# A recurrence's key norms once per 512 tokens, its triangular inverse by 16x16 blocks, and new waits in the plan of TensorE's order

## The chip, the cores and the metric

The kernel runs on one core of a Trainium2 chip. The metric is the device time of one execution in microseconds. A core has TensorE (PE; its weight loads are shown as PEld), VectorE (DVE), ScalarE (ACT), GpSimd (POOL) and SyncE (SP, which issues all DMAs of this kernel). Each engine works through its own instructions in one fixed order. A difference of about 0.2% is what a measurement of this kernel can tell from none.

## The reference

One decoder layer on 2048 tokens of width 1024, in fp32. `h` is the normed input and `z = h @ W_in`. Branch A is RWKV-7 with 8 heads of 64 channels: for each head and token a state `S` is decayed, corrected and read. Branch B is a causal pooling mixer. Both are gated, merged and projected; then come a squared-ReLU MLP, an embedding gate and a norm. The part that the change touches:

```python
kk = heads(k * f32(k_k))
kk = kk / jnp.maximum(jnp.linalg.norm(kk, axis=-1, keepdims=True), L2_EPS)

def rwkv7_step(S, inp):
    r, w, k, v, kk, a = inp
    sa = jnp.einsum('bhvk,bhk->bhv', S, -kk)
    S = (S * w[:, :, None, :]
         + sa[..., None] * (kk * a)[:, :, None, :]
         + v[..., None] * k[:, :, None, :])
    y = jnp.einsum('bhvk,bhk->bhv', S, r)
    return S, y
```

## The kernel before

**Stages.** The tokens are four blocks of 512. Stage A of a block (`stage_A`) makes `z` from the normed input in 128-column pieces; each dense product is three fp32r matmuls (high by high, low by high, high by low parts), and 24 of them fill one PSUM tile `d`. It writes `r|k|v` and the low-rank parts to DRAM as `zD`, and the pooling branch and gates to `thD` and `mbD`. Stage B (`stage_B`) merges the branches and projects them. Then come the MLP and the embedding in two halves of 1024 tokens, which hold no recurrence.

**The recurrence.** It runs in 32 units of 64 tokens, all heads at once: 4 pairs of heads, a pair filling the 128 partitions. Within a unit the steps of 64 tokens are one triangular system, solved by matrices:

- `prep0` loads `zs` from `zD` and makes `kx = k * k_k` and its square `sq`. `prep_a` sums the squares per head (four matmuls with `hsel`), takes `rsqrt` on 8 partitions, and splits the result into `rd`. `prep` spreads it by a matmul with `hbr` and scales `kx`.
- `prep` then makes the products `bdb·AR` (masked by DVE into `Ast`, line 783) and `bdk·AR`, and transposes `bdv` and `BK`. The unit's diagonal blocks of 32x32 go from `Ast` to DRAM (`aD`).
- `invert` loads them as `At`, each 32x32 block on several partitions, and inverts them on DVE: one elimination of pairs of rows (`Apr`), then 16 pairs of a product `Xtmp` (line 869) and a reduction into `Xt` (line 872), over 2, 4, ... 32 columns. `Xt` goes to DRAM (`xD`) and from there in six DMAs into the block-diagonal tile `xd`.
- `chain` is the serial part: `TL·SV` gives `Tn`; `xd·Tn` (even halves) gives `U`; `aof·U` is subtracted from `Tn` by DVE (line 911); `xd·Tn` (odd halves) gives `VU`; `NB·VU` gives the next state `SV`; `RD·SV + Ct·VU` gives the output `Y`. `gnorm` norms `Y` and transposes it (`ybd`).

**What sets the order.** TensorE's order is written out in advance by `drive`: generators for dense work and for the units' parts yield, and a clock in Python (`clock`, advanced by every `mm`) decides which goes on. Behind each step a part yields the time, from the table `LAT`, that must pass on this clock before its next step; dense products fill it. `pace` is the least distance of units. The other engines' orders are set by the framework's scheduler, with the units' instructions at high priority. The recurrence's PSUM tiles come from two rings of two buffers: `rps` (tiles `rp`: all of `prep`) and `cps` (tiles `rc`: `chain`).

Of the kernel before, what the change touches and what calls it, by code (L numbers as in the profile page):

```python
# [10 lines left out]
F32 = mybir.dt.float32  # L11
# [20 lines left out]
NSPLIT = P // (2 * 2 * PC)  # L32
MCOL = SUB // NSPLIT
# [10 lines left out]
           hop=3.1, hu=2.8, hv=5.3, hs=3.0, inv=47.1, gn=17.8, pace=34.4, pace2=31.5)  # L44
# [3 lines left out]
RDK = SUB + 2 * NP  # L48
# [50 lines left out]
def hybrid_kernel(ctx, tc, consts, x, p, g_mix, w_in, mu_shift, w0, w_decay_up, a0, w_aaa_up,  # L99
# [13 lines left out]
    mbD = dram.tile([P, 8, T], F32, name="mbD")  # L113
    yaD = dram.tile([P, NPAIR, T], F32, name="yaD")
# [13 lines left out]
    def mm(out_, lhsT, rhs, start, stop, **kw):  # L128
        n = 1
        for d in rhs.shape[1:]:  # L130
            n *= d
        clock[0] += max(0.107, n * (4 if rhs.dtype == F32 else 1) / 2370.0)
        PE.matmul(out_, lhsT, rhs, start=start, stop=stop, **kw)  # L133
# [62 lines left out]
    with ExitStack() as c1:  # L196
# [136 lines left out]
        ACT.copy(out=bor, in_=raw[:, 0:P])
        hbr = rw.tile([RDK, P], FR, name="hbr")
        POOL.memset(hbr.bitcast(F32), 0.0)
        for o in (0, SUB):
            ACT.copy(out=hbr[o:o + 2 * NP, :], in_=raw[0:2 * NP, P:])
        rd = rw.tile([RDK, W1], FR, name="rd")
        POOL.memset(rd.bitcast(F32), 0.0)
# [5 lines left out]
        bd["aof"] = static([P, PC // 2, P], "aof", 2)  # L345

# [57 lines left out]
        def stage_A(b, nxt):  # L404
# [238 lines left out]
        aD = [dram.tile([4 * PC, SUB, SUB], F32, name=f"aD{i}") for i in range(2)]  # L643
        xD = [dram.tile([4 * PC, SUB, SUB], F32, name=f"xD{i}") for i in range(2)]
# [20 lines left out]
        carried = {}  # L665

        def prep0(i):
# [8 lines left out]
            sq = wt("sq")  # L676
            ACT.activation(out=sq, in_=kx, func=AF.Square)
            return zs, kx, sq

        def prep_a(i):  # L680

            u, g = divmod(i, NG)
            zs, kx, sq = p0.pop(i)
# [7 lines left out]
            ps = rps()  # L691
# [3 lines left out]
            ss = rw.tile([2 * NP, UT], F32, name="kss", bufs=1)  # L695
            DVE.tensor_scalar(ss, ps[0:2 * NP, 0:UT], 1e-24, None, op0=ALU.max)
# [26 lines left out]
            rk2 = rw.tile([P, W1], F32, name="rk2", tag="sq", bufs=1)  # L723
# [6 lines left out]
            return zs, kx, Ei, E, k2, rkr  # L730
# [7 lines left out]
        def prep(i):  # L738
            u, g = divmod(i, NG)
            par = i % 2  # L740
            zs, kx, Ei, E, k2, rkr = pa.pop(i)
# [9 lines left out]
            mm(ps[:, W1:2 * W1], hbr, rd, True, True)  # L751
# [6 lines left out]
            DVE.tensor_tensor(kk, kx, ps[:, W1:2 * W1], ALU.mult)  # L758
# [19 lines left out]

            ps = rps()
# [5 lines left out]
            for h in range(2):  # L785
                for d in range(2):
                    hd = h * 2 + d
                    rows = slice(h * L + d * SUB, h * L + (d + 1) * SUB)
                    SP.dma_start(out=ad[hd * PC:(hd + 1) * PC].rearrange("q s t -> s q t"),  # L789
                                 in_=Ast[rows, :, d * SUB:(d + 1) * SUB])  # L790
            chain_ready[i] = clock[0] + LAT["inv"]
# [38 lines left out]
            xdr = xD[par]  # L830
            for h in range(2):
                for d in range(2):
                    hd = h * 2 + d
                    lo = h * L + d * SUB
                    xv3 = xdr[hd * PC:(hd + 1) * PC].rearrange("q j i -> j q i")
                    for to, fr in ((ALLQ, ALLQ),) if d == 0 else ((EVEN, ODD), (ODD, EVEN)):
                        SP.dma_start(out=xd[lo:lo + SUB, to, lo:lo + SUB], in_=xv3[:, fr, :])
            carried[i] = dict(dl=dl, TL=TL, RD=RD, SV=SV, VU=VU, Ct=Ct, aof=aof, xd=xd, NB=NB, gg=gg, bon=bon)

        def invert(i):  # L840
            par = i % 2
            ad, xdr = aD[par], xD[par]


            Atp = rw.tile([P, SUB * (SUB + 1)], F32, name="At", bufs=1)
            Atf = Atp[:, 0:SUB * SUB]
            At = Atf.rearrange("p (s t) -> p s t", t=SUB)
            SP.dma_start(out=Atf, in_=ad.rearrange("q s t -> q (s t)").unsqueeze(1).broadcast_to(
                [4 * PC, NSPLIT, SUB * SUB]))

            lvl = 1
            while lvl < FS:
                nb = SUB // (2 * lvl)
                Ab = At.rearrange("p s (b r) -> p s b r", r=2 * lvl)
                dgv = Atp.rearrange("p (c w) -> p c w", w=2 * lvl * (SUB + 1))
                for e in range(lvl):
# [150 lines left out]
        def drive(dg):  # L1007
            gate, at, dense_on = None, 0.0, True
            while dense_on or active or counts["gn_done"] < NU:
                admit()  # L1010
                ready = [a for a in active if a[3] <= clock[0] and (a[4] is None or a[4]())]
                if ready:
                    a = min(ready, key=lambda a: (a[0] != "chain", a[3]))
                    a[4] = None
                    try:
                        with tc.high_priority():
                            lat = next(a[2])
                        if lat is None:
# [340 lines left out]
```

## Time and profile before

| | |
|---|---|
| median of 3 runs | 3357.87 us (3354.74 to 3360.87) |
| the profiled execution | 3362.13 us, its span 3360.3 us |
| TensorE's mean granted clock | 0.98 |
| DMA traffic | 485.60 MB, mean 145 GB/s |
| costliest waits on DMA issue | SP for `Xt` before `xD`: 112.6 us in 19 waits |

The profile's page gives busy time by engine; a matmul's end is modelled, so a busy PE is not PE at its peak. In its views a row is: line, engine, operation, output tile <- input tiles, shape, count, then busy us and mean ns of one, then the idle time of the engine just before and what ended it. A wait called "issue" is one for which the profile shows no releaser. A timeline row begins with its start and its length in us, and ends with the idle time ahead of it in brackets.

### The profile page before, as it was taken

How to read it: one execution, taken by the hardware profiler on the slowest of the kernel's cores; microseconds unless marked ns; L12 is line 12 of the kernel's file. 1: busy time of each engine (PE TensorE's matmuls, PEld its weight loads, DVE VectorE, ACT ScalarE, POOL GpSimd, SP SyncE). 2: the span in 40 equal slices, each digit the busy share in tenths (PEclk: the TensorE clock that was granted, in tenths of full speed). 3: DMA queues.
4: the chain of work that ended last, by engine and by line, in shares of the span. 5: the costliest groups of instructions: out<-in, count | busy, mean ns of one | idle time of the engine just before them, and what ended most of it. 6: DMA issues, size and time to landing. Idle time of an engine off the chain costs nothing.

```text
span 3360.3 us, 43232 instructions
## 1 busy us (share of the span) xinstructions
PE 3196.8 (95%) x15177; PEld 2620.5 (78%) x15177; DVE 2021.1 (60%) x5020; ACT 1182.4 (35%) x2406; POOL 950.1 (28%) x1162
## 2 busy tenths in 40 slices
PE   7989999999999997889899999999999999999998
PEld 6777777777878786668688888888788888888887
DVE  4489888788887879873643333333775333333375
ACT  4445544554455444431322222211332222221132
POOL 4655444344434435421111111111102111111110
PEclk9999999999999998999999999999999999999999
DMA  8866767666766567778741111110233111111021
GB/s 249 243 216 205 245 205 236 222 212 186 227 218 219 175 209 235 234 242 290 275 140 51 51 51 51 44 51 26 83 131 113 51 51 51 51 47 47 26 65 60
DMA packets 391030, 485.60 MB, mean 145 GB/s; under 512 B 168158, under 2 KB 298268, under 8 KB 367644
## 3 DMA queue, kind: packets, MB, share of 16 engines
q1 hardware_dynamic: 390812, 482.83, 45.1%
q8 instruction: 120, 1.97, 0.2%
q14 instruction: 98, 0.80, 0.1%
HBM read 363.21 MB, written 119.54 MB: 144 GB/s over the span
## 4 chain that ended last, share of the span: by engine, by line
PE 70%; DVE 14%; DMA 7%; ACT 3%; issue 3%; POOL 2%; SPq 1%; DVEq 0%; POOLq 0%; ACTq 0%
PE d L133 63%; DVE Xtmp L869 3%; PE rc L133 3%; PE rp L133 3%; DMA At<-aD 2%; DVE Xt L872 1%; ACT sq L961 1%; DMA aD<-Ast 1%; DMA wf<-wc 1%; DMA t2k<-yaD 1%; PE rp L137 1%; DVE wf L238 1%; DVE Apr L859 1%; PE rc L137 1%; SPq L789 0%
## 5 line engine op out<-in xcount | busy, mean ns | idle before, releaser
L133 PE MATMUL d<-big,wf 128*128 128x512 f32 (+1 forms) x3288 | 840.6, 403 | 17.6 <-DVE wf L238 9.2
L133 PEld LDWEIGHTS d<-big,wf 128*128 128x128 f32 x3288 | 608.9, 192 | 150.2 <-DVE wf L238 11.7
L133 PE MATMUL d<-wf,rt 128*128 128x512 f32 x3072 | 722.4, 395 | 0.0
L133 PE MATMUL d<-hT,wf 128*128 128x512 f32 x3072 | 700.1, 389 | 0.6 <-DVE hT L185 0.4
L133 PEld LDWEIGHTS d<-wf,rt 128*128 128x128 f32 x3072 | 574.9, 187 | 139.7
L133 PEld LDWEIGHTS d<-hT,wf 128*128 128x128 f32 x3072 | 576.5, 188 | 121.6 <-DVE hT L185 0.7
L1099 POOL TENSOR_TENSOR wf<-wr,wf 128x512 fp32r<-128x512 f32 x146 | 256.8, 1764 | 1396.1 <-ACT wf L1095 1394.5
L1215 DVE TENSOR_TENSOR xa<-xa,d 128x512 f32<-128x512 f32 x256 | 175.7, 686 | 410.0 <-PE d L133 409.6
L1095 ACT CAST wf<-wr 128x1024 fp32r<-128x1024 f32 x148 | 153.4, 1045 | 688.7 <-PE d L133 570.0
L1159 DVE TENSOR_TENSOR t<-t,d 128x512 f32<-128x512 f32 x128 | 87.9, 687 | 274.9 <-ACT t L1158 274.9
L869 DVE TENSOR_TENSOR Xtmp<-Xt,At 128x16 f32<-128x16 f32 (+15 forms) x512 | 238.3, 465 | 9.3
L133 PE MATMUL d<-yx,wf 128*128 128x512 f32 x768 | 210.0, 420 | 25.7 <-ACT yx L387 15.8
L133 PE MATMUL d<-wf,big 128*128 128x512 f32 x768 | 190.5, 401 | 11.0 <-DVE t2k L608 9.2
L1158 ACT ACTIVATE t<-d 128x512 f32<-128x512 f32 x128 | 76.6, 599 | 347.3 <-PE d L133 347.3
L133 PEld LDWEIGHTS d<-yx,wf 128*128 128x128 f32 x768 | 150.1, 202 | 62.1 <-ACT yx L387 17.5
L1099 DVE TENSOR_TENSOR wf<-wr,wf 128x512 fp32r<-128x512 f32 (+1 forms) x148 | 115.8, 783 | 131.3 <-ACT wf L1095 130.9
L133 PE MATMUL d<-wf,hT 128*128 128x512 f32 x768 | 183.6, 394 | 0.0
L1161 DVE TENSOR_TENSOR rt<-t,rt 128x512 fp32r<-128x512 f32 x128 | 154.0, 1203 | 45.3 <-ACT rt L1160 45.3
L133 PEld LDWEIGHTS d<-wf,big 128*128 128x128 f32 x768 | 143.0, 191 | 43.7 <-DVE t2k L608 11.1
L133 PEld LDWEIGHTS d<-wf,hT 128*128 128x128 f32 x768 | 143.9, 188 | 33.6
L872 DVE TENSOR_REDUCE Xt<-Xtmp 128x8 f32<-128x16 f32 (+15 forms) x512 | 147.5, 288 | 9.4
L238 POOL TENSOR_TENSOR wf<-wr,wf 128x640 fp32r<-128x640 f32 (+2 forms) x69 | 121.1, 1756 | 76.4 <-ACT wf L235 71.8
(225 smaller groups left out, 3921.3 us busy)
## 6 DMA issues: line engine op xcount, KB each, us to landing
wf<-wc SPq DMA_DIRECT2D x131, 1024.0 KB, 5.7
wr<-in_w_ff_dram SPq DMA_DIRECT2D x128, 512.0 KB, 4.0
wc<-wf SPq DMA_DIRECT2D x50, 1024.0 KB, 6.3
wr<-in_w_in_dram SPq DMA_DIRECT2D x51, 512.0 KB, 4.4
zD<-t2k SPq DMA_DIRECT2D x96, 256.0 KB, 4.7
zs<-zD SPq DMA_DIRECT2D x32, 640.0 KB, 6.4
At<-aD SPq DMA_DIRECT2D x32, 512.0 KB, 4.8
xt<-in_x_dram SPq DMA_DIRECT2D x28, 512.0 KB, 6.9
```

Source lines behind the costliest of these rows:

```text
L133: PE.matmul(out_, lhsT, rhs, start=start, stop=stop, **kw)
L137: PE.transpose(out_, in_, idn)
L238: eng.tensor_tensor(wf[:, 1, c], raw[:, c], hi.bitcast(F32)[:, c], ALU.subtract)
L859: DVE.tensor_tensor(pr, Ab[:, :, :, e:e + 1].broadcast_to([P, SUB, nb, lvl]), dgv[:, :, o:o + lvl].unsqueeze(1).broadcast_to([P, SUB, nb, ...
L869: DVE.tensor_tensor(tmp[:, :, :, 0:n], Xt[:, :, 0:n].unsqueeze(2).broadcast_to([P, MCOL, FS, n]), At[:, 0:n, r:n].rearrange("p s r -> p r ...
L872: DVE.tensor_reduce(Xt[:, :, r:n].unsqueeze(3), tmp[:, :, :, 0:n], AX.X, ALU.add)
L1095: ACT.copy(out=hi, in_=raw[:, 0:k * n])
L1099: eng.tensor_tensor(wf[:, 1, c], raw[:, c], hi.bitcast(F32)[:, c], ALU.subtract)
L1158: ACT.activation(out=t, in_=ps, func=AF.Relu)
L1159: DVE.tensor_tensor(t, t, ps, ALU.mult)
L1161: DVE.tensor_tensor(rt[:, 1, cs], t, rt[:, 0, cs].bitcast(F32), ALU.subtract)
L1215: DVE.tensor_tensor(xa[j][:, ns], xa[j][:, ns], ps, ALU.add)
```

## The change

Three things change, and with them the plan.

1. **Key norms.** The squares of the keys are taken in stage A, for 512 tokens at once: `key_squares` has the squares as the weight and two columns (`hsel`, now the heads' masks) as the moving operand, `key_norms` takes `rsqrt` of 128x32 values, transposes them and writes 8 rows to DRAM (`kD`). `prep0` reads them back, each row to 64 partitions (`kb`). The per-unit `sq`, `rsqrt` and `rd` go.
2. **The inverse.** Only the 16x16 diagonal blocks are inverted on DVE (8 pairs in place of 16), after 8 small DMAs to `aD` in place of 4. The off-diagonal 16x16 squares (`Of`, masked by POOL from `Ast`) are filled in on TensorE: `Of·Xr` (`Xr` is `Xc` transposed by DVE) is copied into `xd` by ACT with a minus sign, then `ident·Xc + xd·Xc` is copied into `xd` by ACT, in six pieces. `xD` and its DMAs go. `invert` becomes a generator with two steps on TensorE, and both take their PSUM tile from `rps`.
3. **The plan.** `mm` costs an fp32 product max(0.22, n/595) and an fp32r product max(0.11, n/2260); the wait behind `aof·U` is now `ht = 6.5` (it was `hu = 2.8`); `hv` goes from 5.3 to 5.8 and `hs` from 3.0 to 3.5; `inv` is 28.0 up to `Of·Xr`, then `z = 2.8` and `X = 3.5`. A unit's `bdb·AR` may not go ahead of the `Of·Xr` of the unit before.

The diff, cut to its core:

```diff
-LAT = dict(..., hop=3.1, hu=2.8, hv=5.3, hs=3.0, inv=47.1, gn=17.8, pace=34.4, pace2=31.5)
+LAT = dict(..., hop=3.1, hu=2.8, ht=6.5, hv=5.8, hs=3.5, inv=28.0, z=2.8, X=3.5, gn=17.8, pace=34.4, pace2=31.5)
...
-        clock[0] += max(0.107, n * (4 if rhs.dtype == F32 else 1) / 2370.0)
+        clock[0] += max(0.22, n / 595.0) if rhs.dtype == F32 else max(0.11, n / 2260.0)
...
+            def key_squares(j, sq):
+                ps = dps()
+                for c in range(TB // P):
+                    mm(ps[:, 2 * c:2 * c + 2], sq[:, c * P:(c + 1) * P], hsel, True, True)
+                DVE.tensor_scalar(kss[:, :, 2 * j:2 * j + 2], ps[:, 0:n].rearrange("p (c h) -> p c h", h=2), 1e-24, None,
+                                  op0=ALU.max)
+                if j == NPAIR - 1:
+                    late.append(lambda ri=rsqrt(fg, kss.rearrange("p c h -> p (c h)"), TB // P * n, "k", bufs=1): key_norms(ri))
+            def key_norms(ri):
+                ps = dps()
+                for c in range(TB // P):
+                    tr(ps[0:n, c * P:(c + 1) * P], ri[:, c * n:(c + 1) * n], ident)
+                rt = t2k()
+                ACT.copy(out=rt[0:n, :], in_=ps[0:n, :])
+                SP.dma_start(out=kD[:, t0:t0 + TB], in_=rt[0:n, :])
...
+            kb = wt("kb", 2)
+            for h, hp in enumerate(hps):
+                SP.dma_start(out=v3(kb)[hp], in_=kD.rearrange("(j h) t -> h j t", h=2)[h, :, t0:t0 + UT].unsqueeze(
+                    0).broadcast_to([L, NP, UT]))
...
-            for j in range(NP):
-                mm(ps[0:2 * NP, 0:UT], hsel[:, 2 * (NP - 1 - j):2 * (2 * NP - 1 - j)], sq[:, j * UT:(j + 1) * UT],
-                   j == 0, j == NP - 1)
...
-            ri = rsqrt(rw, ss, UT, "k", rows=2 * NP, bufs=1)
...
-            mm(ps[:, W1:2 * W1], hbr, rd, True, True)
...
-            DVE.tensor_tensor(kk, kx, ps[:, W1:2 * W1], ALU.mult)
+            DVE.tensor_tensor(kk, kx, kb, ALU.mult)
...
+            yield lambda: of_read[0] >= i - 1
...
-                    SP.dma_start(out=ad[hd * PC:(hd + 1) * PC].rearrange("q s t -> s q t"),
-                                 in_=Ast[rows, :, d * SUB:(d + 1) * SUB])
+            for b in range(P // SB):
+                SP.dma_start(out=ad[b].rearrange("q s t -> s q t"),
+                             in_=Ast[b * SB:(b + 1) * SB, :, b * SB % L:b * SB % L + SB])
+            Of = bd["Of"][0]
+            for lo in range(0, P, SUB):
+                rows = slice(lo, lo + SUB)
+                POOL.tensor_tensor(Of[rows, :, rows], Ast[rows, :, lo % L:lo % L + SUB],
+                                   omask[rows].unsqueeze(1).broadcast_to([SUB, PC, SUB]), ALU.mult)
...
-            for r in range(0, SUB, FS):
+            for r in range(0, SB, FS):
...
-            SP.dma_start(out=xdr.rearrange("q (k m) i -> (q k) (m i)", m=MCOL), in_=Xt.rearrange("p m i -> p (m i)"))
+            Xc = rw.tile([P, PC, SUB], F32, name="Xc", bufs=1)
+            DVE.tensor_tensor(Xc.rearrange("p q (c t) -> p q c t", t=SB), Xt.unsqueeze(2).broadcast_to([P, PC, 2, SB]),
+                              cmask.unsqueeze(1).unsqueeze(3).broadcast_to([P, PC, 2, SB]), ALU.mult)
+            Xr = rw.tile([P, PC, SUB], F32, name="Xr", tag="Xtmp", bufs=1)
+            DVE.transpose(Xr.rearrange("p q t -> p (q t)"), Xc.rearrange("p q t -> p (q t)"))
+            yield LAT["inv"]
+            Of, xd = bd["Of"][0], bd["xd"][par]
+            yield lambda: counts["chain_done"] >= i - 1
+            ps = rps()
+            for q in range(PC):
+                mm(ps[:, q * SUB:(q + 1) * SUB], Of[:, q, :], Xr[:, q, :], True, True)
+            for lo in range(0, P, SUB):
+                ACT.activation(out=xd[lo:lo + SUB, :, lo:lo + SUB], in_=v3(ps[:, 0:PC * SUB], SUB)[lo:lo + SUB],
+                               func=AF.Copy, scale=-1.0)
+            of_read[0] = i
+            yield LAT["z"]
+            ps = rps()
+            mm(ps[:, 0:PC * SUB], ident, Xc.rearrange("p q t -> p (q t)"), True, False)
+            for q in range(PC):
+                mm(ps[:, q * SUB:(q + 1) * SUB], xd[:, q, :], Xc[:, q, :], False, q == PC - 1)
+            pv = v3(ps[:, 0:PC * SUB], SUB)
+            for lo in range(0, P, SUB):
+                for to, fr in ((ALLQ, ALLQ),) if lo % L == 0 else ((EVEN, ODD), (ODD, EVEN)):
+                    ACT.copy(out=xd[lo:lo + SUB, to, lo:lo + SUB], in_=pv[lo:lo + SUB, fr, :])
+            chain_ready[i] = clock[0] + LAT["X"]
...
             DVE.tensor_tensor(Tn, Tn, ps[:, 0:W1], ALU.subtract)
-            yield LAT["hu"]
+            yield LAT["ht"]
```

The order of instructions moves in three places. In these rows a tile's name carries its number, a matmul's inputs are the moving and then the stationary operand, and x is how many of a kind follow each other.

TensorE, from `aof·U` to the second `xd·Tn` of a unit in the midst of stage A, first as it was:

```order
L133 MATMUL rc<-U,aof_242 128x128 x2
L133 MATMUL d<-big,wf 128x512 x12
L133 MATMUL d<-yx,wf 128x512 x3
L133 MATMUL rc<-Tn,xd_236 128x128 x2
L133 MATMUL d<-yx,wf 128x512 x9
```

The same place of another unit in stage A now:

```order
L130 MATMUL rc<-U,aof_239 128x128 x2
L130 MATMUL d<-yx,lrw 128x512 x3
L130 MATMUL d<-big,wf 128x512 x6
L134 MATMUL rp<-ident,ybd_235 128x128 x4
L130 MATMUL d<-big,wf 128x512 x18
L130 MATMUL rc<-Tn,xd_233 128x128 x2
```

Fifteen dense products stood between the two; now 27 do, and the transposes of `ybd`.

TensorE around `bdb` and `bdk`, which take the two buffers `rp` in turn, before:

```order
L133 MATMUL d<-big,wf 128x512 x9
L133 MATMUL rp<-AR,bdb_226 128x128 x4
L133 MATMUL d<-big,wf 128x512 x3
L133 MATMUL rp<-AR,bdk_228 128x128 x4
L133 MATMUL d<-big,wf 128x512 x12
L137 MATMUL rp<-ident,bdv_230 128x128 x4
```

And now, with the two new steps of `invert` ahead of them:

```order
L130 MATMUL rp<-Xr,Of_241 128x32 x4
L130 MATMUL d<-yx,lrw 128x512 x3
L130 MATMUL d<-big,wf 128x512 x12
L130 MATMUL rp<-Xc,ident 128x128
L130 MATMUL rp<-Xc,xd_231 128x32 x4
L130 MATMUL rp<-AR,bdb_221 128x128 x4
L130 MATMUL rp<-AR,bdk_223 128x128 x4
L130 MATMUL d<-big,wf 128x512 x9
```

`bdk` took the buffer that `bor` had filled some way ahead; now it takes the one that `xd·Xc` has filled just ahead of `bdb`. In 20 of the 32 units the three stand in this order in the ring.

DVE around the subtraction that makes the second `Tn` of a unit (line 911), before:

```order
L872 TENSOR_REDUCE Xt<-Xtmp 128x4x2
L869 TENSOR_TENSOR Xtmp<-Xt,At 128x8x30
L872 TENSOR_REDUCE Xt<-Xtmp 128x4x2
L869 TENSOR_TENSOR Xtmp<-Xt,At 128x256
L911 TENSOR_TENSOR Tn<-Tn,rc 128x256
L872 TENSOR_REDUCE Xt<-Xtmp 128x4x2
```

And now (the subtraction is line 936):

```order
L859 TENSOR_TENSOR Apr<-At 128x392
L861 TENSOR_TENSOR At<-At,Apr 128x4x14x7
L450 SCALAR_TENSOR_TENSOR t2k<-ze,vec,t2k 128x512
L936 TENSOR_TENSOR Tn<-Tn,rc 128x256
L862 MEMSET At 128x4x16
L868 TENSOR_TENSOR Xtmp<-Xt,At 128x8x2
```

It stood behind ten or more of the 16 products of the next unit's inverse in 24 of 32 units; now it stands ahead of that inverse or near its head, in 18 units behind `Apr`, which is the first to wait for the DMA of `At`.

More of the change, by code (lines that the diff above doesn't have):

```diff
@@ L31 @@
 SUB = 32
-NSPLIT = P // (2 * 2 * PC)
-MCOL = SUB // NSPLIT
+SB = SUB // 2
 TB = 512
@@ L327, in static @@
             return r
-        raw = fg.tile([P, 2 * P], F32, name="craw", tag="t2k", bufs=5)
+        raw = fg.tile([P, P], F32, name="craw", tag="t2k", bufs=5)
         SP.dma_start(out=raw, in_=consts[:, C_BO:])
         bor = rw.tile([P, P], FR, name="bor")
[L333 to L339, printed above, removed]
+        ACT.copy(out=bor, in_=raw)
         bd = {}
@@ L480, in stage_A @@
                 which, j = divmod(zi, NPAIR)
+                if late:
+                    late.pop(0)()
+                    yield
+                if which == 1:
+                    sq = t2k()
+                    ACT.activation(out=sq, in_=zs, func=AF.Square, scale=col("kk", j))
+                    late.append(lambda j=j, sq=sq: key_squares(j, sq))
                 ps = dps()
@@ L740, in prep @@
             par = i % 2
-            zs, kx, Ei, E, k2, rkr = pa.pop(i)
+            zs, kx, kb, Ei, E, k2, rkr = pa.pop(i)
             r_ = zs[:, 0:NP, :]
@@ L841, in invert @@
             par = i % 2
[L842 to L856, printed above, removed]
-                    pr = rw.tile([P, SUB, nb, lvl], F32, name="Apr", tag="Xtmp", bufs=1)
-                    o = e * SUB + lvl
-                    DVE.tensor_tensor(pr, Ab[:, :, :, e:e + 1].broadcast_to([P, SUB, nb, lvl]),
-                                      dgv[:, :, o:o + lvl].unsqueeze(1).broadcast_to([P, SUB, nb, lvl]), ALU.mult)
-                    DVE.tensor_tensor(Ab[:, :, :, lvl:2 * lvl], Ab[:, :, :, lvl:2 * lvl], pr, ALU.add)
-                lvl *= 2
@@ L863, in invert @@
-            DVE.memset(Atf[:, 0:SUB * SUB:SUB + 1], 1.0)
-            Xt = rw.tile([P, MCOL, SUB], F32, name="Xt", bufs=1)
-            POOL.tensor_copy(Xt.rearrange("p m i -> p (m i)"), x0t)
-            tmp = rw.tile([P, MCOL, FS, SUB], F32, name="Xtmp", tag="Xtmp", bufs=1)
-            for r in range(0, SUB, FS):
+            Atf = rw.tile([P, PC * SB * SB], F32, name="At", bufs=1)
+            SP.dma_start(out=Atf, in_=aD[par].rearrange("b q s t -> b (q s t)").unsqueeze(1).broadcast_to(
+                [P // SB, SB, PC * SB * SB]))
@@ new lines, in invert @@
+            At = Atf.rearrange("p (q s t) -> p q s t", q=PC, t=SB)
+            Ad = Atf.rearrange("p (q w) -> p q w", q=PC)
+            nb = SB // FS
+            Ab = Atf.rearrange("p (q s b r) -> p q s b r", q=PC, s=SB, r=FS)
+            ns = SB - FS
+            pr = rw.tile([P, PC, ns, nb - 1], F32, name="Apr", tag="Xtmp", bufs=1)
+            step = FS * (SB + 1)
+            DVE.tensor_tensor(pr, Ab[:, :, 0:ns, 1:, 0], Ad[:, :, step + 1:SB * SB - SB:step].unsqueeze(2).broadcast_to(
+                [P, PC, ns, nb - 1]), ALU.mult)
```

106 lines of the change are left out of this document (45 added, 61 removed).

## The prediction

> **What bounds the kernel now.** I read the head of the page first, then busy time by stretch. The columns of the second view are the stretch and its length in us, then busy time and instructions of PE, PEld, DVE, ACT, POOL, and last the granted clock of PE, the DMA share and GB/s.
>
> ```profile
> span 3360.3 us, 43232 instructions
> PE 3196.8 (95%) x15177; PEld 2620.5 (78%) x15177; DVE 2021.1 (60%) x5020; ACT 1182.4 (35%) x2406; POOL 950.1 (28%) x1162
> ```
>
> ```profile
> 160.00:1290.00 1130.00, 1055.58 (x5577) 873.28 (x5575) 949.43 (x2771) 584.81 (x1362) 495.22 (x779) 0.97 0.68 213
> 1290.00:1600.00 310.00, 263.60 (x1294) 216.66 (x1294) 221.46 (x555) 107.54 (x253) 102.25 (x117) 0.93 0.76 254
> 1764.00:3361.00 1597.00, 1584.47 (x6985) 1290.05 (x6983) 689.67 (x1343) 370.46 (x599) 241.16 (x137) 1.00 0.19 58
> ```
>
> TensorE is the bound, and its instructions run in one fixed order. Behind 1764 us it idles 13 of 1597 us at full clock; the change does not touch that part. Between 160 and 1600 us, where the 32 units of the recurrence run between the dense products of stages A and B, PE idles 74 + 46 = 120 us, its clock is below 1, and DVE is 84% busy in the first stretch. So time can come only from PE's idle gaps there and the slow clock behind them; whatever TensorE is given to do in addition is paid in full. Next, who ended the gaps: the waits of PE (us in total, times, longest), and the grouped row of the chain's products with `xd` (busy, mean ns, then idle before).
>
> ```profile
> PE d L133 <- DVE t2k L608: 16.1, 6, 6.9
> PE d L133 <- DVE wf L238: 9.2, 4, 4.6
> PE rc L133 <- DVE VU L918: 9.0, 3, 5.8
> ```
>
> ```profile
> L133 PE MATMUL rc<-Tn,xd 128*128 128x128 f32 x256 | 44.5, 300 | 55.0 <-issue 34.4 <-DMA xd<-xD 10.2 <-ACT zp L509 4.9
> ```
>
> The largest wait, 55 us, stands before `xd·Tn`, and its releaser is mostly unnamed ("issue"). The timeline of one unit names it:
>
> ```profile
> 940.30 0.61 PE L133 MATMUL rc<-U,aof 128*128 128x128 f32 x4
> 945.56 0.68 PE L133 MATMUL rc<-Tn,xd 128*128 128x128 f32 x4 [1.21 <-issue]
> 944.10 1.03 DVE L869 TENSOR_TENSOR Xtmp<-Xt,At 128x256 f32<-128x256 f32 x1
> 945.05 0.41 DVE L911 TENSOR_TENSOR Tn<-Tn,rc 128x256 f32<-128x256 f32 x1
> ```
>
> `aof·U` is over at about 940.7, but the subtraction that makes the new `Tn` starts at 945.05: it stands in DVE's queue behind the inverse of the next unit (16 pairs of L869 and L872). The plan gives this hop 2.8 us of other matmuls. So PE waits for DVE's order, not for arithmetic.
>
> **The change, part by part.** Sums are against the profiled execution: 3362.1 us, of which the span is 3360.3; the median shown, 3357.9, is 4.3 lower.
>
> *1. TensorE's own work.* In the timeline the next start gives a group's cost; an fp32 product leaves two records, so x8 is four products.
>
> ```profile
> 600.92 0.61 PE L133 MATMUL rp<-sq,cst 128*8 128x64 f32 x8
> 601.46 0.66 PE L137 MATMUL rp<-ident,BK 128*128 128x128 f32 x4
> ...
> 626.36 4.38 PE L133 MATMUL d<-big,wf 128*128 128x512 f32 x18
> 630.58 0.40 PE L133 MATMUL rp<-rkr,bor 128*128 128x256 f32 x2
> 630.91 0.38 PE L133 MATMUL rp<-rd,hbr 40*128 40x256 f32 x1
> 631.22 1.97 PE L137 MATMUL d<-ident,xt 128*128 128x128 f32 x16
> ...
> 637.28 1.06 PE L133 MATMUL rp<-AR,bdb 128*128 128x128 f32 x8
> 638.09 0.94 PE L133 MATMUL d<-yx,wf 128*128 128x512 f32 x3
> ```
>
> ```profile
> L133 PEld LDWEIGHTS rp<-sq,cst 128*8 128x8 f32 x256 | 13.8, 89 | 10.4 <-issue 9.9 <-DVE gss L949 0.4
> L133 PEld LDWEIGHTS rc<-SV,RD 128*128 128x128 f32 x256 | 39.5, 195 | 0.0
> ```
>
> Removed per unit: `sq` 0.54 and `rd` 0.31 us. Added per unit: four `Of·Xr`, one with `ident`, four `xd·Xc`: 9 products, 18 records. No row has a 128-column weight with only 32 moving columns. From below it is half of a `sq` record (0.54/8/2 = 0.034 us: half the columns), from above a `bor` record (0.33/2 = 0.165). I take the `bdb` record, 0.81/8 = 0.101, because the weight is as wide, and the load of 128 columns takes 195 - 89 = 106 ns more than that of 8: narrow moving data does not make the load cheaper. That is 18 x 0.101 - 0.85 = +0.97 us, +31 in 32 units. Key norms per block: 16 products with 2 columns and four transposes (0.49, a quarter of the 1.97 us row), 32 x 0.101 + 0.49 = 3.7, four blocks +15. **+46** (ends -2 and +91).
>
> [...]
>
> *2. The hop before the second `xd`.* `ht` is 6.5 where `hu` gave 2.8: mostly 27 dense products stand there in place of 15, work that is due anyway, so the wait costs nothing as long as dense work is left. And in the new DVE order `Tn` stands at the head of the next inverse or before it, where it stood behind ten or more pairs in most units. I leave 6 of the 55 us; the 10.2 for the `xd` DMA goes with `xD`: **-49** (-55 to -35).
>
> *3. The clock behind the gaps.*
>
> ```profile
> 705.25 0.68 PE L133 MATMUL rc<-Tn,xd 128*128 128x128 f32 x4 [3.51 <-issue]
> 705.69 5.97 PE L133 MATMUL d<-big,wf 128*128 128x512 f32 x18
> 711.50 0.40 PE L133 MATMUL rp<-rkr,bor 128*128 128x256 f32 x2
> ```
>
> 18 dense products take 630.58 - 626.36 = 4.22 us undisturbed (part 1) and 711.50 - 705.69 = 5.81 behind a gap of 3.5 us: 1.6 more. Thirteen gaps of 2 us or more go by parts 2 and 5 (nine at the second `xd`, the DMA's, three of the waits for DVE): **-21** (-30 to -8).
>
> [...]
>
> *4. A new wait: the PSUM ring `rp`, two buffers.* In 20 of 32 units the order is: `xd·Xc` into one buffer, the four `bdb` into the other, then `bdk`, which needs the first again. Six ACT copies must have read it; before, `bdk` followed `rkr·bor`, long drained. ACT's rows:
>
> ```profile
> 892.33 3.70 PE L133 MATMUL d<-big,wf 128*128 128x512 f32 x15
> 892.61 0.75 ACT L887 COPY Tn<-rc 64x256 f32<-64x256 f32 x2 [0.46 <-PE rc L133]
> 897.90 1.06 ACT L906 COPY VU<-rc 32x128 f32<-32x128 f32 x4
> ```
>
> ACT starts 0.28 us after PE moves on; a copy of 32x128 takes 0.265; two such and four of half the columns, at 0.2 (an estimate between half and whole), make 0.28 + 1.33 = 1.6, with the semaphore back some 1.8. PE has 0.81 (`bdb`) to hide it. Behind `bdk` wait `bdv`, the next chain step and all dense work. **+20** (20 x 1.0; 0 to 42, the upper end with one 0.5-us and longer instruction ahead on ACT).
>
> *5. DVE's load.* Busy us and mean ns of one:
>
> ```profile
> L869 DVE TENSOR_TENSOR Xtmp<-Xt,At 128x16 f32<-128x16 f32 (+15 forms) x512 | 238.3, 465 | 9.3
> L872 DVE TENSOR_REDUCE Xt<-Xtmp 128x8 f32<-128x16 f32 (+15 forms) x512 | 147.5, 288 | 9.4
> L155 DVE SCALAR_TENSOR_TENSOR rs_yk<-rs_qk,rs_yk 8x64 f32<-8x64 f32 x96 | 27.3, 284 | 0.2
> ```
>
> The sixteen pairs of a unit take (238.3 + 147.5)/32 = 12.1 us. The eight of 144 to 256 elements go, those of 16 to 128 stay; they are more than half of it, and I take 7.5 us. So go the nine steps of the key rsqrt, 9 x 0.28 = 2.5; the product for `Xc` and the transpose come, some 0.5 each (128 elements, near the mean of the first row). About -9 a unit, some 290 us of the 1171 in the two stretches. It shortens no path of its own; it shows in the waits for DVE. Of 16.1 + 9.0 = 25.1 us of PE's waits I let two thirds go, since most of that queue was the inverse: **-17** (-25 to 0). SP no longer stands waiting for `Xt` with weight loads behind it, so of the 9.2 us for `wf` half goes: **-5** (-9 to 0). POOL (four small products for `Of`, the `rd` product gone) and ACT (ten copies, some 2.4 us a unit, one square gone) stay near half busy; what they delay is in part 4.
>
> *6. The new inverse's path.* First SP, then DVE, then PE:
>
> ```profile
> 879.37 2.27 SPq L789 DMA_DIRECT2D aD<-Ast  x4
> 892.72 1.13 DVE L859 TENSOR_TENSOR Apr<-At 128x512 f32<-128x512 f32 x1
> 910.43 0.42 DVE L872 TENSOR_REDUCE Xt<-Xtmp 128x8 f32<-128x256 f32 x1
> 877.18 1.05 PE L133 MATMUL rp<-AR,bdb 128*128 128x128 f32 x8
> 1271.47 1.05 PE L133 MATMUL rp<-AR,bdb 128*128 128x128 f32 x8
> 1296.29 1.13 DVE L859 TENSOR_TENSOR Apr<-At 128x512 f32<-128x512 f32 x1
> ```
>
> Here `Apr` starts 15.5 us after `bdb`, and the block ends 18.1 later with other work between. Eight pieces to `aD` in place of four delay it by 2.3; the block loses 7.5 and the key steps between: about 9 remain. So `Xr` is ready some 27 us behind `bdb`; in the new order some 93 dense products at 0.234 (4.22/18), 22 us, and 8 us of the recurrence's own groups stand between `bdb` and `Of·Xr`. In stage B it is not enough: at 1271 `Apr` came 24.8 behind. Four units there could wait 7 us each; DVE's shorter queue, in which that `Apr` stood, takes part of it: **+8** (0 to 40).
>
> Sum: 46 - 49 - 21 + 20 - 17 - 5 + 8 = **-18**: 3344 for the profiled execution, **3340** on the scale of the median.
>
> **The rivals.** *The DMA at DVE's head (slower).* In 18 units `Tn` now stands behind `Apr`, which waits for `At`. `aof·U` comes 33 dense products and some 5 us of small groups behind the next `bdb`, 13 us, and the second `xd` 7 later; so an `At` beyond some 20 us stalls PE there, and `Of·Xr` behind it. Against it: 15.5 above, plus 2.3. For it: 24.8 in stage B. At 22.5 everywhere 18 units pay 2.5 us: that is 45 us more, 3385. *The loads cost more (slower).* At the `bor` record, 0.165, term 1 is +91 in place of +46: 3385; it decides from 0.127 a record on, where 704 added records have eaten the 18 us. *Nothing is won.* The ring's `bdk` waits 2 us in place of 1, behind an ACT cast or activation: +20, 3360, no change. *More is won.* Term 1 near 20 since the moving columns are few, and no late `Xr`: some -52 in all, 3306. That the shorter inverse does nothing and only `ht` works is possible: then the -17 falls away and the time is 3357.
>
> **How the numbers follow.** Forecast 0.45; more won 0.15; no change, by either way, 0.15; the DMA at DVE's head 0.13; dear loads 0.12. A measurement tells about 0.2% (7 us) from no change. Faster 0.60, same 0.15, slower 0.25. The range leaves out a tail on each side: 3292 to 3384; the likeliest case alone is 3318 to 3351.
>
> **What would show it.** Right: PE's idle before `Tn,xd` falls from 55 to under 10; `rp` products with `Of`, `ident` and `xd` add some 58 us of PE work, near 0.1 a record; DVE falls by some 300 us; PE waits before `bdk` for ACT's `xd` copies, about 1 us, 20 times. Wrong: `Apr <- DMA At` grows far beyond its present share and `Tn` starts behind it; `Of·Xr` waits for `Xr` outside stage B; records of 0.16; or `bdk` waits of 2 us and more.

## The result and the profile after

The changed kernel takes 3496.18 us (median of 4 runs, 3492.57 to 3499.65) against 3357.70 of the kernel before: ratio **1.041** (95% interval 1.039 to 1.043). It is 4.1% slower, 156 us above the forecast of 3340 and above the range (3292 to 3384).

The head of its page, and busy time by stretch (the columns are those of the prediction):

```profile
span 3490.8 us, 43424 instructions
...
PE 3263.9 (94%) x15609; PEld 2694.0 (77%) x15609; DVE 1759.6 (50%) x4124; ACT 1256.5 (36%) x2712; POOL 941.2 (27%) x1257
```

```profile
160.00:1290.00 1130.00, 996.12 (x5331) 839.28 (x5330) 675.80 (x1841) 597.47 (x1493) 451.75 (x792) 0.94 0.63 190
...
1895.00:3491.00 1596.00, 1583.84 (x6980) 1289.17 (x6978) 686.30 (x1343) 370.67 (x599) 241.12 (x137) 1.00 0.18 58
```

The last stretch is as it was (13 us idle of some 1597), so the 130 us that the span grew stand ahead of it, where the recurrence runs. There TensorE did less in the same 1130 us (996 us busy, 1056 before) at a clock of 0.94 (0.97), although DVE was busy for 676 us in place of 949. By the head, the span grew by 130.5 us: 67.1 us of TensorE's busy time and 63.4 of its idle time (226.9 against 163.5 us).

The groups of TensorE and then of DVE that answer to the prediction (busy us, mean ns | idle ahead of them and what ended it):

```profile
L130 PE MATMUL rc<-Tn,xd 128*128 128x128 f32 x256 | 42.5, 291 | 32.1 <-ACT Tn L912 21.1 <-DVE At L862 6.2 <-DVE Tn L936 2.9
L130 PE MATMUL rp<-AR,bdk 128*128 128x128 f32 x256 | 37.3, 291 | 13.2 <-ACT xd L897 9.8 <-ACT sq L986 3.0 <-POOL rk L734 0.4
...
L130 PE MATMUL rp<-Xc,xd 128*128 128x32 f32 x256 | 32.2, 270 | 5.1 <-ACT xd L886 5.1
L130 PE MATMUL rp<-Xr,Of 128*128 128x32 f32 x256 | 31.3, 266 | 0.0
...
L130 PE MATMUL rp<-Xc,ident 128*128 128x128 f32 x64 | 12.4, 276 | 3.1 <-DVE Ast L793 3.1
...
L859 DVE TENSOR_TENSOR Apr<-At 128x392 f32<-128x392 f32 x32 | 29.1, 909 | 220.5 <-DMA At<-aD 220.5
```

The releaser "issue" ahead of `rc<-Tn,xd` is gone, but 32.1 of the 55.0 us are still there: 21.1 ahead of the first `xd·Tn` of two units, for ACT's copy `Tn`, and 11.0 in all ahead of the second (44.9 before). What stands out is the last row: DVE stood **220.5 us** at `Apr`, 6.9 per unit on average, for the load of `At`. Before, the same row said:

```profile
L859 DVE TENSOR_TENSOR Apr<-At 128x512 f32<-128x512 f32 x32 | 40.6, 1268 | 51.6 <-DMA At<-aD 51.4
```

One unit of the changed kernel, with a wait longer than the average, shows the path, SP first, then DVE (start, length):

```profile
589.21 7.15 SPq L796 DMA_DIRECT2D aD<-Ast  x8
596.46 0.38 SPq L840 DMA_DIRECT2D gg<-zD  x1
596.94 0.58 SPq L990 DMA_DIRECT2D yaD<-sq  x1
597.61 1.28 SPq L698 DMA_DIRECT2D kb<-kD  x2
599.06 0.60 SPq L849 DMA_DIRECT2D At<-aD  x1
...
588.49 0.69 DVE L793 TENSOR_TENSOR Ast<-rp,mk 128x512 f32<-128x512 f32 x1
...
611.31 0.91 DVE L859 TENSOR_TENSOR Apr<-At 128x392 f32<-128x392 f32 x1 [8.86 <-DMA At<-aD]
```

`Ast` is done at 589.2, the eight pieces are issued by 596.4, `At` goes out at 599.1, and `Apr` starts 12.2 us later (median of the 32 units 8.2). DVE has nothing it may do for 8.9 us of that, since its order is fixed; dense evictions stand behind `Apr`. In the page's chain of the work that ended last, the load of `At` has 5% of the span; before it had 2%. Finally some of TensorE's longest waits:

```profile
PE d L130 <- DMA wf<-wc: 31.0, 11, 7.8
PE rc L130 <- ACT Tn L912: 21.1, 2, 11.2
...
PE d L130 <- DVE t2k L629: 19.2, 6, 5.7
```

The first was 2.5 us before, the last 16.1. Summed over all rows of TensorE, the idle time ahead of the chain's products (tiles `rc`) fell from 74.8 to 53.1 us; ahead of the units' other products (`rp`) it rose from 4.3 to 28.8, and ahead of dense work (`d`) from 75.1 to 135.9.

### The profile page after: what moved, and what is told of

Its sections match the earlier page's. It is cut to its first block, busy times and chain, and to the rows that moved or that the text cites. A ratio compares the mean times of both kernels' runs of the same rounds, so it can differ in the third digit from the quotient of the medians.

```text
span 3490.8 us, 43424 instructions
## 1 busy us (share of the span) xinstructions
PE 3263.9 (94%) x15609; PEld 2694.0 (77%) x15609; DVE 1759.6 (50%) x4124; ACT 1256.5 (36%) x2712; POOL 941.2 (27%) x1257
## 4 chain that ended last, share of the span: by engine, by line
PE 66%; DMA 15%; DVE 8%; ACT 3%; issue 3%; POOL 3%; SPq 1%; DVEq 0%; POOLq 0%; ACTq 0%
PE d L130 60%; DMA At<-aD 5%; PE rp L130 3%; PE rc L130 2%; DMA wf<-wc 2%; DMA zs<-zD 1%; DMA aD<-Ast 1%; ACT sq L986 1%; DVE bdb L772 1%; DMA t2k<-thD 1%; DMA zD<-t2k 1%; DMA wc<-wf 1%; SPq L796 1%; DVE Xtmp L868 1%; PE rc L134 1%
## 5 line engine op out<-in xcount | busy, mean ns | idle before, releaser
L130 PE MATMUL d<-big,wf 128*128 128x512 f32 (+1 forms) x3288 | 854.5, 409 | 50.8 <-DMA wf<-wc 30.4
L130 PEld LDWEIGHTS d<-big,wf 128*128 128x128 f32 x3288 | 620.5, 196 | 186.5 <-DMA wf<-wc 35.3
L130 PE MATMUL d<-yx,wf 128*128 128x512 f32 x768 | 205.1, 414 | 32.8 <-ACT yx L379 12.9
L130 PE MATMUL d<-wf,big 128*128 128x512 f32 x768 | 193.1, 406 | 22.7 <-DVE t2k L629 19.2
L859 DVE TENSOR_TENSOR Apr<-At 128x392 f32<-128x392 f32 x32 | 29.1, 909 | 220.5 <-DMA At<-aD 220.5
L986 ACT ACTIVATE sq<-rp,vec 64x64 f32<-64x64 f32 x256 | 102.5, 401 | 60.1 <-PE rp L134 56.9
```

The lines of the kernel that those rows point to most:

```text
L986: ACT.activation(out=yo[hp, q * UT:(q + 1) * UT], in_=ps[hp, q * P:(q + 1) * P][:, hp], func=AF.Identity, scale=col("lnw", q)[hp], bias=co ...
```

## The experiments

Each ratio is against the kernel before as it was measured beside that kernel (medians 3358 to 3365 us); the text gives its 95% interval. Idle is span less TensorE's busy time, of the profiled execution.

| kernel | us | ratio | PE busy | PE idle | DVE's wait at `Apr` |
|---|---|---|---|---|---|
| before | 3357.7 | 1 | 3196.8 | 163.5 | 51.6 |
| changed | 3496.2 | 1.041 | 3263.9 | 226.9 | 220.5 |
| norms_alone | 3430.7 | 1.020 | 3196.8 | 233.4 | 90.8 |
| inverse_alone | 3454.6 | 1.027 | 3279.8 | 176.3 | 145.2 |
| plan_alone | 3410.9 | 1.014 | 3214.6 | 192.3 | 47.1 |
| ht_alone | 3387.9 | 1.007 | 3211.5 | 178.7 | 38.9 |
| price_alone | 3418.8 | 1.016 | 3210.0 | 205.0 | 61.8 |
| at_k8 | 3410.9 | 1.014 | 3211.0 | 199.0 | 114.1 |
| at_free | 3439.4 | 1.023 | 3249.0 | 190.1 | 20.0 |

**The parts alone.** First one part at a time on the kernel before, or, for the inverse, the change without the norms.

```diff
 # norms_alone: before, with key_squares, key_norms and kb; no sq, rsqrt, rd in the unit
-            DVE.tensor_tensor(kk, kx, ps[:, W1:2 * W1], ALU.mult)
+            DVE.tensor_tensor(kk, kx, kb, ALU.mult)
 # inverse_alone: the changed kernel with the reverse of this
```

> The kernel before with only the key norms moved to stage A (squares and inverse roots once per 512 tokens, kD, two kb loads a unit); old inverse, old plan constants. Theory 'DVE stands at Apr until At lands' (220.5 us there in the changed kernel, 51.4 before): the norms have little to do with it, 3340 to 3365 us, Apr's wait 40 to 80 us. Rival 'the two kb loads a unit fill SP's queue and make aD and At late': 3390 us or more, Apr's wait over 120 us. Rival 'the plan's constants alone': no change, 3358.

> The changed kernel with the key norms put back into each unit (no kss, kD or kb; the old rsqrt, rh, rl and rd). Theory 'DVE stands at Apr': nearly all of the loss stays, 3460 to 3510 us, with Apr's wait 180 us or more. Rival 'kb loads': it goes back to 3350 to 3400. Rival 'TensorE's added work alone' (62 us by the groups' busy time, of which the norms' squares and transposes are 18 against 32 removed): 3400 to 3430, with PE idle near the 163.5 us of before.

```diff
 # plan_alone: before
-           hop=3.1, hu=2.8, hv=5.3, hs=3.0, inv=47.1, gn=17.8, pace=34.4, pace2=31.5)
+           hop=3.1, hu=2.8, ht=6.5, hv=5.8, hs=3.5, inv=47.1, gn=17.8, pace=34.4, pace2=31.5)
-        clock[0] += max(0.107, n * (4 if rhs.dtype == F32 else 1) / 2370.0)
+        clock[0] += max(0.22, n / 595.0) if rhs.dtype == F32 else max(0.11, n / 2260.0)
```

> The kernel before with only the planner's numbers changed: prices of a matmul (0.22 us and n/595 for fp32, 0.11 and n/2260 for fp32r), 6.5 us for the wait between aof.U and the second xd.Tn (2.8 before), hv 5.8, hs 3.5; inv stays 47.1. Theory 'DVE stands at Apr' and theory 'TensorE's added work': the 55 us of TensorE's idle time ahead of rc<-Tn,xd shrink below 25 and the time falls to 3310 to 3350. Rival 'the new constants space TensorE's order badly' (dense work gets late): 3380 or more.

Measured: norms 1.020 (1.018 to 1.022), inverse with its plan 1.027 (1.025 to 1.029), plan 1.014 (1.012 to 1.016). Every part loses by itself. The norms lose 68 us, though they leave TensorE's busy time as it was and take 35 us from DVE and 52 from POOL: the rival's time, with a wait at `Apr` (90.8) that neither theory had. The plan's numbers add nothing and lose 48, as their rival had it. inverse_alone keeps two thirds of the loss, not nearly all: 3454.6 us is below its theory's range, and so is the wait at `Apr`. Its span is 96 us longer than before: 83 of them are TensorE's busy time (576 more records, and a mean clock of 0.976 in place of 0.980), and only 13 are idle time, although DVE stood 145.2 us at `Apr`. So a wait of DVE is not by itself a loss of the kernel.

**At's load.** Then the load of `At` in the changed kernel, in another shape, and without its dependence:

```diff
 # at_eight: the changed kernel
-            SP.dma_start(out=Atf, in_=aD[par].rearrange("b q s t -> b (q s t)").unsqueeze(1).broadcast_to(
-                [P // SB, SB, PC * SB * SB]))
+            for b in range(P // SB):
+                SP.dma_start(out=Atf[b * SB:(b + 1) * SB, :], in_=aD[par][b].rearrange("q s t -> (q s t)").unsqueeze(
+                    0).broadcast_to([SB, PC * SB * SB]))
 # at_free: the changed kernel
-            SP.dma_start(out=Atf, in_=aD[par].rearrange("b q s t -> b (q s t)").unsqueeze(1).broadcast_to(
+            SP.dma_start(out=Atf, in_=w_in[0][0:P // SB, 0:PC * SB * SB].unsqueeze(1).broadcast_to(
```

> The changed kernel with At loaded by eight DMAs, one for each block of 16 rows (16 copies of one 4 KB row each), in place of one of 8 rows x 16 copies; the same bytes, 7 more issues of about 0.5 us a unit on SP. Theory 'At's one DMA with 8 outer rows lands late' (8.2 us median from its issue to Apr, 5.6 before with 16 outer rows x 8 copies): Apr starts 5 to 6 us after the last issue, its wait falls below 170 us, and the time falls by 15 to 50 us, to 3445 to 3480. Rival 'it is the number of issues on SP and the landing of aD that make At late': Apr's wait grows to 260 us or more and the time is 3500 to 3560.

> The changed kernel with At loaded from an input (the first 8 rows of w_in, the same 512 KB in the same shape, 8 rows x 16 copies) and not from aD, so that Apr no longer waits for Ast, the eight writes and their landing; aD is still written. The inverses are those of other blocks. Theory 'DVE's 220.5 us of standing at Apr is most of the loss': the wait falls below 40 us and the time to 3420 or less. Rival 'TensorE's added records and the clock are most of it': 3450 to 3490, with DVE's wait gone all the same.

at_eight: 3459.1 us, ratio 1.029 (1.027 to 1.032), 37 us below the changed kernel; inside the expectation of the late load, in spite of 7 more issues a unit:

```profile
L860 DVE TENSOR_TENSOR Apr<-At 128x392 f32<-128x392 f32 x32 | 30.4, 949 | 157.1 <-DMA At<-aD 126.3 <-DMA mbD<-t2k 27.6 <-DMA zD<-t2k 2.2
```

at_free: 3439.4, 1.023 (1.020 to 1.026):

```profile
L859 DVE TENSOR_TENSOR Apr<-At 128x392 f32<-128x392 f32 x32 | 33.9, 1060 | 20.0 <-PE rp L130 11.6 <-DMA At<-in_w_in_dram 8.3
```

The wait is nearly gone and 57 of the 138 us are won: between the two expectations, a large term, but not "most of the loss". TensorE's order is the same in both kernels, but those of DVE, ACT, POOL and SP are not (`At` now goes out some 33 us ahead of the unit's first write to `aD`, where it went out 7 behind it, and `Apr` moves ahead with it), so the 57 us are the worth of the whole edit; how much of it is DVE's standing at `Apr` alone is not shown. The eight rows were then put into the kernel before, where no engine's order changes by it:

```diff
 # at_k8: before
-            SP.dma_start(out=Atf, in_=ad.rearrange("q s t -> q (s t)").unsqueeze(1).broadcast_to(
-                [4 * PC, NSPLIT, SUB * SUB]))
+            SP.dma_start(out=Atf, in_=ad[0:4 * PC:2].rearrange("q s t -> q (s t)").unsqueeze(1).broadcast_to(
+                [2 * PC, 2 * NSPLIT, SUB * SUB]))
```

> The kernel before with At loaded from every second of the 16 rows of aD, 16 copies of each, in place of all 16 rows 8 times: the same 512 KB in pieces of 4 KB, one instruction, the same order on every engine; half of the inverses are those of other blocks. Theory '8 outer rows land later than 16' (8.2 us against 5.6 in the two kernels): from At's issue to Apr 8 us or more, Apr's wait 51.4 to 100 us or more, and the time up by 10 to 40 us, to 3368 to 3400. Rival 'what At's load does late in the changed kernel comes from the queue behind the eight writes': 5.6 us, and 3350 to 3370.

```profile
L859 DVE TENSOR_TENSOR Apr<-At 128x512 f32<-128x512 f32 x32 | 40.7, 1273 | 114.1 <-DMA At<-aD 114.0
```

3410.9 us, 1.014 (1.012 to 1.016): **47 us, beyond the upper end, from the shape of one load.** Where DVE waited for it, `Apr` starts 4.7 us after the issue with 16 rows (median of 21 waits) and 7.5 with 8 (28 waits). The last `Apr` starts 48 us later than before, so the whole loss arises while the units run. This is the clearest run of the study.

**The plan's numbers, apart.**

```diff
 # ht_alone: before
-            yield LAT["hu"]
+            yield LAT["ht"]      # 6.5, behind aof.U
 # price_alone: before, with the two prices of a matmul of the change; price_scaled: also all of LAT times 1.05
```

> The kernel before with one number changed: 6.5 us in place of 2.8 planned between aof.U and the second xd.Tn. The prediction's step (49 of the 55.0 us ahead of rc<-Tn,xd are won): 3300 to 3325 us. Rival 'the idle time only moves, because DVE, ACT and the weights' DMAs are as late as before and something else waits for them': the 34.4 us of issue go, others come, 3345 to 3420.

> The kernel before with the planner's two prices of a matmul changed and nothing else (an fp32r matmul of 512 columns 0.227 us in place of 0.216, an fp32 one never under 0.22). The prediction gave the prices no cost: 3350 to 3370 us. Rival 'the prices thin out the dense work that is planned beside a unit, by about 5 per cent, and cost what all the constants together cost (3410.9)': 3390 to 3420, with fewer TensorE records in 420-1290 than before's 4356.

ht_alone: 1.007 (1.004 to 1.010). Its row for `xd·Tn`, and some of its waits:

```profile
L133 PE MATMUL rc<-Tn,xd 128*128 128x128 f32 x256 | 41.5, 287 | 6.4 <-ACT Tn L887 4.1 <-ACT sq L961 1.8 <-DMA xd<-xD 0.5
```

```profile
PE rc L133 <- DVE VU L918: 17.9, 9, 5.5
...
PE d L133 <- ACT wf L235: 12.4, 3, 8.1
...
PE d L133 <- DVE t2k L633: 11.2, 4, 5.2
PE rp L133 <- DVE RD L803: 10.9, 6, 2.7
PE rp L137 <- DVE RD L803: 9.7, 4, 7.2
```

The 55.0 us fall to 6.4, and still the kernel is 27 us slower, as the rival had it: these five rows alone are 62.1 us, 20.4 before (the second `RD` row was 3.1, the first was not there). TensorE's order shows where the filling came from. Behind `aof·U` of the 32 units stand 919 records into `d` in place of 450; between the last product of a unit's chain and the first of the next, where most of the next unit's other products stand, 1256 in place of 1710; ahead of `NB·VU` 761 in place of 789. The idle time ahead of `rc` falls from 74.8 to 33.6 us, but ahead of `rp` it rises from 4.3 to 29.6 and ahead of `d` from 75.1 to 105.9. In sum the span has 15.2 us more idle time, and 14.7 more busy time for the same 15177 records, at a mean clock of 0.977 in place of 0.980.

price_alone: 1.016 (1.014 to 1.019), as much as all the constants together, as its rival had it. Between 160 and 1290 us TensorE gets through 5372 records, where before it got through 5577:

```profile
160.00:1290.00 1130.00, 1023.10 (x5372) 843.73 (x5371) 933.37 (x2709) 568.29 (x1329) 473.50 (x757) 0.96 0.66 205
```

> The kernel price_alone (3418.8 us) with all planned waits multiplied by 1.05, as the price of a dense matmul was (0.227 against 0.216), so that about as many dense matmuls stand between the steps of a unit as before. Theory 'the prices cost because they thin the dense work beside the units': back to 3355 to 3385. Rival 'any other order than that of before loses 40 us or more': 3400 to 3425.

price_scaled: 3381.8, 1.004 (1.003 to 1.006), with 5504 records, inside the expectation of the theory. The scaled waits win 41 of the 58 us back. The prices cost mainly because every wait in the plan is counted in them, so that a dearer dense product means fewer of them in the same planned wait. Last, in the changed kernel the old prices and waits:

```diff
 # old_plan: the changed kernel, with the mm line of before and
-           hu=2.8, ht=6.5, hv=5.8, hs=3.5,
+           hu=2.8, ht=2.8, hv=5.3, hs=3.0,
```

> The changed kernel with the old prices of a matmul and the old waits (2.8 for ht, hv 5.3, hs 3.0); inv 28.0, z and X stay, since only the new inverse has them. Theory 'the plan's numbers cost the same 48 us here as alone': 3440 to 3455 us. Rival 'they fit the new inverse and cost nothing here': 3490 to 3510, with PE's idle time ahead of rc<-Tn,xd back at 50 us or more.

3511.1, 1.044 (1.041 to 1.047), outside both expectations, the rival's by 1 us; its 60.0 us of idle time ahead of `rc<-Tn,xd` are the rival's. Here the new numbers gain about 15 us. The same numbers lose 48 beside the old inverse; their worth depends on the rest.

**How narrow the order of before is.**

```diff
 # pace_up, pace_dn: before; after_up, after_dn: the changed kernel, by 1.5
-pace=34.4, pace2=31.5)
+pace=34.9, pace2=32.0)      # pace_dn: 33.9, 31.0
```

> The kernel before with the planned distance of two units 0.5 us longer (34.9 and 32.0 in place of 34.4 and 31.5): the same instructions on every engine, dense matmuls moved by one to three places against the units. Theory 'the numbers of before are a narrow optimum of its order, and every change of the order loses some tens of us until they are set anew': 3380 to 3420 us, though nothing is added. Rival 'each part of the change has a cost of its own': 3350 to 3370.

> The same 0.5 us shorter (33.9 and 31.0). Narrow optimum: 3380 to 3420 us on this side too. Each part has its own cost: 3350 to 3370.

> The changed kernel with the distance of two units 1.5 us longer (35.9 and 33.0). Narrow optimum, and the changed kernel's numbers are not at theirs: the time moves by 15 us or more in some direction, and one of this and the next comes out below 3480. Each part has its own cost, independent of the order: within 15 us of 3496.

> The changed kernel with the distance of two units 1.5 us shorter (32.9 and 30.0). As for the longer one: moves of 15 us or more, below 3480 in one of the two, by the narrow optimum; within 15 us of 3496 otherwise.

pace_up 3381.4, 1.006 (1.004 to 1.007), and pace_dn 3388.0, 1.008 (1.006 to 1.010): both signs lose, 18 and 24 us, with not one instruction added. Both are inside the expectation of the narrow optimum, 3381.4 just so. The changed kernel goes to 3491.9 (1.038, 1.036 to 1.040; no clear difference) and 3466.9 (1.032, 1.030 to 1.034), 29 us better at the shorter distance: it is not at the best of its numbers. So some 20 us can go by merely moving this order, and ht_alone (27) and price_scaled (17) lose no more than about that.

> The changed kernel with two edits that each gained: At in eight loads (3459.1) and the distance of two units 1.5 us shorter (3466.9). If the gains come from separate causes they add: 3420 to 3440. If both only move the order about its optimum: 3445 to 3490.

eight_dn, both edits that gained: 3450.1, 1.026 (1.023 to 1.028), inside the second expectation. The gains of 37 and 29 do not add; 46 of the 66 remain. It is the fastest form of the whole change that still inverts its own blocks, and far above before.

**The norms' 68 us.**

```diff
 # kb_alone: before
+            kb = wt("kb", 1, NP * 48)
+            for h, hp in enumerate(hps):
+                SP.dma_start(out=v3(kb, 48)[hp], in_=zD[0:2 * NP, 0, :].rearrange("(j h) t -> h j t", h=2)[
+                    h, :, t0:t0 + 48].unsqueeze(0).broadcast_to([L, NP, 48]))
 # norms_no_kb: norms_alone without the loads
-            return zs, kx, kb
+            return zs, kx, kb1      # a tile of zeros
 # norms_kb3: norms_alone
-            kb = wt("kb", 2)
+            kb = wt("kb", 3)
```

> The kernel before with two loads a unit added that nobody reads (rows of zD broadcast to 64 partitions, 48 of 64 columns, as the two kb loads of the changed kernel), norms as before. Theory 'the two kb loads cost SP and the DMA queues what the norms alone lost (68 us)': 3400 to 3430. Rival 'a shift of the order is what the norms lost, and the loads are small': 3365 to 3395, like the half microsecond of pace.

> The kernel norms_alone (3430.7 us) without its two kb loads a unit: kx is multiplied by a tile of zeros, so the keys of the recurrence are zero. Theory 'kb loads': it falls to 3360 to 3395, and Apr's wait from 90.7 us toward 51. Rival 'order and stage A': 3410 to 3435.

> The kernel norms_alone (3430.7 us) with a third buffer for kb, so that its loads seldom wait on SP for the kx of two units before (there SP stood 56 us ahead of kb's loads in 150-1480). Theory 'kb's loads block SP, what is queued behind them (zs, aD, At, weights) lands later, and DVE stands at Apr': Apr's wait falls from 90.7 us to 60 or less and the time to 3365 to 3400. Rival 'the loads cost by their own transfer': 3420 to 3435.

kb_alone 3370.1, 1.0016 (1.0003 to 1.0029); norms_no_kb 3366.8, 1.0008 (0.9994 to 1.0022); norms_kb3 3438.7, 1.021 (1.019 to 1.023). TensorE's order is the same in norms_alone and norms_no_kb; `Apr`'s rows, of norms_alone and then of norms_no_kb:

```profile
L868 DVE TENSOR_TENSOR Apr<-At 128x512 f32<-128x512 f32 x32 | 38.0, 1188 | 90.8 <-DMA At<-aD 90.7
```

```profile
L866 DVE TENSOR_TENSOR Apr<-At 128x512 f32<-128x512 f32 x32 | 37.3, 1166 | 19.8 <-DMA At<-aD 19.4
```

With the loads, DVE stands 71 us longer at `Apr` and the kernel takes 64 us more, though `kb` itself is waited for only once, 0.8 us. Loads that nobody reads cost 7, as the rival had it. The theory of the blocked buffer fell with norms_kb3, which is no faster than norms_alone (`Apr` 91.2). The load of `At` itself is no slower (4.8 us from issue to `Apr` where DVE waited, 5.0 without `kb`); it goes out later, 7.5 us behind the first write to `aD` in place of 4.6 (medians). In 12 of 32 units of norms_alone `kb`'s issues stand on SP between that write and `At`, 18 us in all, and SP waits 72.2 us for the landing of `aD` ahead of `At`, 32.8 without `kb`. Why SP has longer to wait there stays open: the reader of `kb` also makes the scheduler order DVE and SP anew, and norms_no_kb has zeros for keys.

## Why the prediction was wrong

- **The bound was right:** TensorE, in a fixed order; the MLP's part did not move.
- **Part 1, TensorE's added work, +46: right.** By the prediction's own measure, the start of what comes next, a record costs 0.102 us (0.812 for the eight of `Of·Xr` and of `xd·Xc`, medians of 32 units) in place of 0.101. The weight loads of `Of·Xr` and `xd·Xc`, with 32 moving columns, took 191 and 196 ns, those of `bdb·AR`, with 128, took 192 (means): narrow moving data did not make them cheaper. By busy time the three groups are 75.9 us for 576 records, 0.132 each, but a group's busy time runs on behind the start of the next group, and the `bdb` row of the prediction gives the same 1.06/8 = 0.132. In at_free, at nearly the clock of before (0.979), TensorE has 52 us more busy time, near the 46; the 67 of the changed kernel hold a slower clock besides (0.971). In this unit the next group starts 0.81 us behind:

```profile
631.30 0.98 PE L130 MATMUL rp<-Xr,Of 128*128 128x32 f32 x8
632.11 3.01 PE L130 MATMUL d<-yx,wf 128*128 128x512 f32 x12
```

- **Part 2, the hop before the second `xd`, -49: this step failed.** Ahead of that product the idle time did fall, from 44.9 to 11.0 us, and in ht_alone 6.4 of the 55.0 were left, where 6 were predicted. What was wrong is the sentence that the wait "costs nothing as long as dense work is left". Dense products are work that is due, but they are also what covers the other waits of the unit. The products put into this hop were taken from the stretch between one chain and the next, and the idle time came back ahead of the units' other products and of dense work: in ht_alone the gain of 49 became a loss of 27. Whether these 27 are the hop's own or the price of moving the order was not separated; that the 49 were not won is shown.
- **Part 3, the clock, -21: it went the other way,** with parts 2 and 5. Behind the 3.5 us gap of the kernel before that it quotes, the granted clock was 0.61 from 705.69 to 708.50 us and 0.80 from there to 711.50, where the undisturbed 18 products had 1.00. The mean granted clock fell from 0.980 to 0.971 while TensorE idled more; by these means and the two spans that is some 34 us of full-clock time lost (an estimate: 0.029 x 3491 less 0.020 x 3360).
- **Part 4, the ring, +20:** PE waits ahead of `bdk` for ACT's copies 13 times, 9.8 us in all. Right in kind, half the size. The 0.2 us that it gave the semaphore had no row; in these 13 waits the first weight load of `bdk` starts 0.05 us behind the end of the last copy (median).
- **Part 5, DVE's load, -22: nothing of it came.** DVE's busy time fell by 261 us, near the 290, but DVE stood 169 us more at `Apr`. TensorE waited as long as before for DVE's evictions (`t2k` 19.2 us, 16.1 before), for `VU` (11.2, 9.0) and for `wf` (9.2 both times).
- **Part 6, the new inverse's path, +8: this failed too.** It gave the four more pieces 2.3 us and kept the load itself as it was. The pieces took 3.2 us more (5.2 in place of 2.0 from the first issue to the end of the last, means), and the load landed 3.5 us later (8.2 from issue to `Apr` where DVE waited, 4.7 before). `Of·Xr` itself never waited. That DVE would stand at `Apr` for `At` was the first rival, which had 0.13; it saw the cost at the second `xd`, through `Tn` behind `Apr`, but there only 11.0 us of idle time stand in all. So that its price of 45 us is near the 57 of at_free is luck.
- **What had no term at all:** the two prices and `kb`'s loads. Beside the old inverse they cost 58 and 64 us alone; in the changed kernel the new numbers of the plan gained 15 (old_plan), and taking the norms out gained 42 (inverse_alone).

So the sum fails in two ways: the gains of parts 2, 3 and 5 did not come, and the load of `At` had no cost in it. This load is shown as a cause with a size in the kernel before, 47 us; in the changed kernel the edit that frees `Apr` from its block's own writes won 57. Of the 79 us that remain in at_free, 52 are TensorE's busy time, nearly all of it added work; the last 27 are idle time scattered over a dozen waits. That a neutral half microsecond costs 18 to 24 us shows that the old order was a narrow optimum; how much of these 27 is lost tuning and how much the change's own, was not separated.

## What to carry to other kernels

When every engine runs in a fixed order, a wait that is filled is not a wait that is won: ask where the filling came from. Shift one planning number by a neutral half microsecond first, to see what a mere move of the order costs. Compare a group's cost in one measure only, by busy time or by the next start. Look at the outermost dimension of every load on a critical path before and after an edit; the same bytes in eight rows were worth 47 us. A price in a planner is the unit of all its waits, so rescale these together.

## What the runs showed of the hardware

The load of 512 KB from 8 rows, 16 copies each, needs 7.5 us from issue to use where 16 rows, 8 copies each, need 4.7 (medians where DVE waited), and its issue holds SP for 0.604 us in place of 0.536 (medians of at_k8 and before). Eight loads of one row each (at_eight) go out in some 0.41 us apiece, with a median landing of 2.3 us. Why the load from 8 rows takes longer, no run shows.
